# Low parts, sums of squares and gate sums of a two-layer hybrid block, moved from GpSimd to VectorE

## The chip, the cores and the metric

The kernel runs on one core of a Trainium2 chip. The metric is the device time of one launch, in microseconds (us): the median of three runs. The engines are called PE (TensorE: its matmuls; PEld is its weight load), DVE (VectorE), ACT (ScalarE), POOL (GpSimd) and SP (SyncE, which issues most of the transfers; a q behind an engine's name means its sequencer or queue).

## What is computed

One step of a diffusion transformer with two layers (D 1024, feed-forward width 2816) on 1024 latent tokens and 256 context tokens. Cut to the parts that the change touches:

```python
def rmsnorm(x, w):
    y = x * lax.rsqrt(jnp.mean(x * x, axis=-1, keepdims=True) + EPS)
    return y * w

def trunk_layer(x, mod, lp, ctx):
    sh1, sc1, g1, sh2, sc2, g2 = mod
    h = rmsnorm(x, lp['norm1_w']) * (1 + sc1) + sh1
    p = h @ lp['w_in']
    ...                                  # attention, RG-LRU scan, Hyena long convolution
    mix = jnp.concatenate([att, lru, hy], axis=-1)
    x = x + g1 * (mix @ lp['w_out'])
    h2 = rmsnorm(x, lp['norm2_w']) * (1 + sc2) + sh2
    x = x + g2 * ((jax.nn.silu(h2 @ lp['ffn_w1']) * (h2 @ lp['ffn_w3'])) @ lp['ffn_w2'])
    ...
```

The context tokens go through the same layer, with the same weights and a conditioning of their own.

## The kernel before, in words

**Products in two parts.** Every large matmul is made from three: each float32 operand is cut into a high part (rounded to fp32r) and a low part (what the rounding left), and `mm3` (L153 to L156) adds high by high (L154), high by low (L155) and low by high (L156) in PSUM. `split` (L158 to L161) makes the parts: ACT copies the high part (L160), then another engine subtracts it from the source and so writes the low part (L161). Which engine does that is the call's argument, DVE if there is none. The low part waits for the copy, and PE for both.

**Stages, in order, with the time of the profiled execution.** Loads, norm and modulation (0 to 106 us); `w_in` of layer 0 (to 400); filter spectra and Hyena (to 600); context mix and latent attention (to 958); `w_out` (to 1085); the quarters of the feed-forward operands (to 1130); ffn_up (to 1650); ffn_down (to 1955), with the norms of layer 1 in it; `w_in` of layer 1 (to 2200); Hyena and attention (to 2664); `w_out` (to 2800); quarters (to 2850); ffn_up (to 3350); ffn_down (to 3676).

**Weights.** `wtile` loads 128x1024 floats into a tile wst (3 buffers) and splits it into a tile whl (4 buffers; L161 on POOL). `w_in` and `w_out` use it.

**Norms.** `ss_add` squares on ACT (L360) and adds into two sums: one in three on DVE, the others on POOL (L362). `norm` scales each of the eight row blocks on DVE (L402); for even blocks ACT writes the high part with the bias and DVE the low part (L404, L405), for odd blocks ACT adds the bias, then copies the high part, and POOL subtracts (L160, L161).

**Feed-forward.** The products of the latents are done by a scheme of seven products of quarter size in place of eight. `quarters` (L510 to L554) forms the sums of the quarters of the normed latents on DVE (L538 to L547) and cuts each into its parts (`cut`, L526 to L528): of the 28 cuts, 12 are on DVE and 16 on POOL. In each of the 11 passes of `ffn_up` four weight tiles come in; each pair gives four splits of 128x1024 (w0, w1, wb, wa; L161 on POOL), DVE makes the weight sums between them (L628, L629, L633, L634), drains the products from PSUM (L622, L637 to L648) and computes the gates (L612, L614). At the end of a pass five sums of two gates (L656, on POOL) go to memory with two single gates (L657): sums 0, 3 and 6 through a tile gs with one buffer, 2 and 5 through slots of a tile e.

`ffn_down` has seven products of 11 passes each. A pass loads one or two 128x512 weight tiles (L694) and a gate sum (L700), adds two weights on DVE (L706), splits the result (A: L161 on POOL) and the gate sum (B: L161 on DVE), and PE does twelve matmuls of 512 columns. Passes with context work also split both weights (C, on POOL) and the context gates (gk, on DVE).

**Order.** The Tile framework's scheduler with its own timeline simulation sets the order on each engine (`TCARGS`). Each engine runs its instructions in that order; a semaphore holds one until what it reads is there and what it overwrites has been read. Buffers in pools come free in the same way. Line numbers after the change are lower by 4 from about L414 on, by 1 at L405.

## Time and profile before

| | |
|---|---|
| Median of three runs | 3681.47 us (3678.79 to 3682.36) |
| The profiled execution, its own time | 3678.18 us |
| Its span, first to last instruction | 3676.4 us |
| Mean granted clock of PE | 0.971 |
| Busy: PE, PEld | 3476.9 us (95%), 2758.4 us (75%) |
| Busy: DVE, ACT, POOL | 2331.1 us (63%), 1430.7 us (39%), 1444.6 us (39%) |
| L161 on POOL, output whl | 898.3 us in 463 instructions |

A busy share is an average over stages with different limits, and a busy PE is not PE at its peak. The time that can be won is in PE's gaps, and which engine ends a gap differs by stage. One core runs, so its span is the time but for some 2 us around it.

### The profile page before, as it was taken

What the parts mean: (1) busy time and instruction counts of PE and PEld (TensorE: products, weight loads), DVE (VectorE), ACT (ScalarE), POOL (GpSimd) and SP (SyncE); (2) the same over time, 40 slices, a digit from 0 to 9 for tenths busy, and PEclk for the clock granted to TensorE, in tenths of its full rate; (3) what the DMA queues carried; (4) which work ended last, traced back from release to release, by engine and by line L of the source; (5) the groups of instructions that cost most, each with busy time, mean ns of one, the idle gap of its engine ahead of it and who ended that gap; (6) DMA issues with size and microseconds to landing.
All of it is one profiled execution on the core that took longest, in us unless ns stands there. A gap on an engine that the chain in (4) does not pass through costs nothing.

```text
span 3676.4 us, 49838 instructions
## 1 busy us (share of the span) xinstructions
PE 3476.9 (95%) x18198; PEld 2758.4 (75%) x18198; DVE 2331.1 (63%) x4016; ACT 1430.7 (39%) x2347; POOL 1444.6 (39%) x940
## 2 busy tenths in 40 slices
PE   6989988999999999999999999989998999999998
PEld 3657776667777888887777778767686888888777
DVE  6544577887466655665685673777638556565666
ACT  4333333655342222224544542455524222222443
POOL 3333034110145555547654332310035555455664
PEclk7999998999999999999999999999998999999999
DMA  7565573310411222226675336430141222224667
GB/s 273 175 202 164 201 277 107 121 48 23 138 52 63 89 78 92 78 90 231 191 238 182 106 117 203 153 108 28 36 151 36 84 92 78 77 92 157 205 205 244
DMA packets 402331, 485.89 MB, mean 132 GB/s; under 512 B 38542, under 2 KB 251072, under 8 KB 398758
## 3 DMA queue, kind: packets, MB, share of 16 engines
q1 hardware_dynamic: 398950, 468.03, 38.7%
q0 software_dynamic: 3136, 14.68, 1.2%
q8 instruction: 143, 2.34, 0.3%
q14 instruction: 102, 0.84, 0.1%
HBM read 350.94 MB, written 131.67 MB: 131 GB/s over the span
## 4 chain that ended last, share of the span: by engine, by line
PE 60%; DVE 7%; DMA 6%; issue 5%; POOL 4%; ACT 2%; SPq 1%; DVEq 0%; POOLq 0%; ACTq 0%
PE pu L155 8%; PE pu L156 8%; PE pu L154 8%; PE pvo L966 4%; PE sps L931 4%; PE tps L947 4%; POOL whl L161 3%; PE puv L155 2%; PE puv L154 2%; PE puv L156 2%; PE ops L155 2%; PE ops L156 2%; PE ops L154 2%; DMA wst<-in_ffn_w_dram 2%; PE py L154 2%
## 5 line engine op out<-in xcount | busy, mean ns | idle before, releaser
L161 POOL TENSOR_TENSOR whl<-wst,whl 128x512 fp32r<-128x512 f32 (+1 forms) x463 | 898.3, 1950 | 866.5 <-ACT whl L160 833.6
L160 ACT ACTIVATE whl<-wst 128x512 fp32r<-128x512 f32 (+1 forms) x488 | 394.2, 825 | 846.2 <-PE pu L156 277.9
L154 PE MATMUL pu<-hq,whl 128*128 128x512 f32 x1232 | 489.6, 399 | 7.6 <-ACT hq L527 6.2
L156 PE MATMUL pu<-hq,whl 128*128 128x512 f32 x1232 | 488.8, 398 | 0.0
L154 PE MATMUL wps<-h,whl 128*128 128x512 f32 (+1 forms) x768 | 289.3, 377 | 2.9 <-ACT h L404 1.7
L155 PE MATMUL pu<-hq,whl 128*128 128x512 f32 x704 | 280.8, 399 | 8.4 <-POOL hq L528 4.8
L156 PE MATMUL wps<-h,whl 128*128 128x512 f32 (+1 forms) x768 | 287.9, 376 | 0.0
L155 PE MATMUL wps<-h,whl 128*128 128x512 f32 (+1 forms) x768 | 285.0, 371 | 1.7 <-POOL h L161 1.2
L154 PEld LDWEIGHTS pu<-hq,whl 128*128 128x128 f32 x1232 | 234.1, 190 | 63.0 <-ACT hq L527 8.1
L156 PEld LDWEIGHTS pu<-hq,whl 128*128 128x128 f32 x1232 | 234.4, 190 | 54.9
L154 PE MATMUL py<-whl 128*128 128x512 f32 x616 | 225.1, 399 | 14.3 <-ACT whl L160 8.9
L155 PE MATMUL py<-whl 128*128 128x512 f32 x616 | 228.5, 395 | 0.1
L156 PE MATMUL py<-whl 128*128 128x512 f32 x616 | 220.5, 394 | 1.6 <-POOL whl L161 1.6
L155 PE MATMUL pu<-hl,whl 128*128 128x512 f32 x528 | 210.9, 400 | 8.8 <-POOL hl L528 8.8
L934 ACT ACTIVATE pq<-pq,mn 128x1280 f32<-128x1280 f32 (+1 forms) x160 | 190.2, 1189 | 66.3 <-DVE pq L932 64.0
L947 PE MATMUL tps<-ident,pq 128*128 128x128 f32 x1344 | 198.7, 279 | 16.0 <-ACT pk L951 6.2
L156 PE MATMUL puv<-h,whl 128*128 128x256 f32 x704 | 200.4, 285 | 4.6 <-POOL whl L161 4.6
L154 PE MATMUL puv<-h,whl 128*128 128x256 f32 x704 | 200.1, 284 | 1.4 <-ACT whl L160 1.4
L706 DVE TENSOR_TENSOR wst<-wst 128x512 f32<-128x512 f32 x110 | 137.1, 1247 | 99.5 <-POOL whl L161 63.4
L155 PE MATMUL puv<-h,whl 128*128 128x256 f32 x704 | 200.0, 284 | 0.0
L947 PEld LDWEIGHTS tps<-ident,pq 128*128 128x128 f32 x1344 | 158.4, 143 | 52.4 <-DVE pk L949 18.1
L932 DVE TENSOR_SCALAR_CACHE_REDUCE pq<-sps,mn 128x512 f32<-128x512 f32 (+1 forms) x256 | 156.4, 612 | 46.7 <-PE sps L931 43.2
(355 smaller groups left out, 8038.1 us busy)
## 6 DMA issues: line engine op xcount, KB each, us to landing
wst<-in_ffn_w_dram SPq DMA_DIRECT2D x264, 256.0 KB
wst<-in_ffn_w_dram SPq DMA_DIRECT2D x88, 512.0 KB
wst<-in_w_mod_dram SPq DMA_DIRECT2D x68, 512.0 KB
gr<-gd_l SPq DMA_DIRECT2D x132, 256.0 KB
gd_l<-gs SPq DMA_DIRECT2D x66, 256.0 KB
wst<-in_w_in_dram SPq DMA_DIRECT2D x32, 512.0 KB
wst<-in_w_mod_dram SPq DMA_DIRECT2D x14, 1024.0 KB
gd_l<-g SPq DMA_DIRECT2D x44, 256.0 KB
```

The costliest lines, as they stand in the source:

```text
L154: mm(ps, wh, xh, start=first, stop=False)
L155: mm(ps, wh, xl, start=False, stop=False)
L156: mm(ps, wl, xh, start=False, stop=last)
L160: nc.scalar.activation(hi, src, AF.Copy)
L161: (eng or nc.vector).tensor_tensor(lo, src, hi.bitcast(F32), ALU.subtract)
L706: nc.vector.tensor_tensor(st[:, 0], st[:, 0], st[:, 1], op)
L931: nc.tensor.matmul(p, qx[:, ts], kt[:, h, k0:k0 + kn], start=h == 0, stop=h == 1)
L932: nc.vector.tensor_scalar(pt[:, k0:k0 + kn], p, -1.0, mn[:, c - 1:c] if c else BIG, ALU.mult, ALU.min, accum_out=mn[:, c:c + 1])
L934: nc.scalar.activation(pt, pt, AF.Exp, bias=mn[:, len(chunks) - 1:], scale=-1.0, accum_out=ls[:, t:t + 1])
L947: nc.tensor.transpose(ps[:, k, t], pq[t][:, (t0 + k) * 128:(t0 + k + 1) * 128], self.ident)
L966: nc.tensor.matmul(ob[64 * hd:64 * hd + 64, 0], vx[:, t], pk[:, t].rearrange("p t q -> p (t q)"), start=t == nkt - 1, stop=t == 0)
```

## The change

Everything that the norms, `w_in`, `w_out`, the quarters and both feed-forward stages did on GpSimd goes to VectorE: 463 low parts of weights (221 of 128x1024, 242 of 128x512), 32 low parts of odd norm blocks, 45 sums of squares, 32 cuts of quarters and 110 sums of gates, 682 instructions. The odd norm blocks now go the way of the even ones, so that ACT does one pass for each instead of two (32 fewer) and DVE's low part takes the bias in the same instruction. POOL keeps the filter, rotary, scan and convolution work and its transfers.

```diff
--- before.py
+++ after.py
@@ -359,7 +359,7 @@
                 sq = self.rows(list(xs.shape))
             nc.scalar.activation(sq, xs, AF.Square)
             h = 0 if d % three == 0 else 1
-            (nc.gpsimd if h else nc.vector).tensor_tensor(ss[:, h], ss[:, h], sq, ALU.add)
+            nc.vector.tensor_tensor(ss[:, h], ss[:, h], sq, ALU.add)
 
     def h_new(self, s, bi, hp):
         s.h[bi] = []
@@ -400,24 +400,20 @@
             A, B = self.nA[l][j][:, s.cond, d:d + 1], self.mod(l, s, 3 * j, d)
             t = tp.tile([128, N], F32, tag="ft", name="nt", bufs=FT)
             nc.vector.scalar_tensor_tensor(t, self.xs(s, bi, d), A, p2, ALU.mult, ALU.mult)
-            if d % 2 == 0:
-                nc.scalar.activation(hh, t, AF.Identity, bias=B)
-                nc.vector.scalar_tensor_tensor(hl, t, B, hh.bitcast(F32), ALU.add, ALU.subtract)
-            else:
-                nc.scalar.activation(t, t, AF.Identity, bias=B)
-                self.split(t, hh, hl, nc.gpsimd)
-
-    def wtile(self, src, shp=(8, 128), eng=None):
+            nc.scalar.activation(hh, t, AF.Identity, bias=B)
+            nc.vector.scalar_tensor_tensor(hl, t, B, hh.bitcast(F32), ALU.add, ALU.subtract)
+
+    def wtile(self, src, shp=(8, 128)):
         nc = self.nc
         st = self.wp.tile([128, *shp], F32, tag="wst", name="wst", bufs=SBUFS)
         nc.sync.dma_start(st, src)
         w = self.wp.tile([128, 2, *shp], F32R, tag="whl", name="whl", bufs=WBUFS)
-        self.split(st, w[:, 0], w[:, 1], eng or nc.gpsimd)
+        self.split(st, w[:, 0], w[:, 1])
         return w
 
-    def w_in_w(self, l, i, eng=None):
+    def w_in_w(self, l, i):
         m = MORDER[i]
-        return self.wtile(self.a["w_in"][l][:, m * 128:(m + 1) * 128].rearrange("(k p) m -> p k m", p=128), eng=eng)
+        return self.wtile(self.a["w_in"][l][:, m * 128:(m + 1) * 128].rearrange("(k p) m -> p k m", p=128))
 
     def w_in(self, l, pool, fill):
         nc = self.nc
@@ -431,7 +427,7 @@
             ws = []
             for i in g:
                 fill(i)
-                ws.append(self.w_in_w(l, i, nc.vector if l == 0 and i < 3 else None))
+                ws.append(self.w_in_w(l, i))
             es = {i: [] for i in g}
             for b in self.all:
                 s, bi, b0, N = b
@@ -514,7 +510,7 @@
         ha, hb, _ = hp
         b11, b21 = self.lat.x[0]
         b12, b22 = self.lat.x[1]
-        V, G = nc.vector, nc.gpsimd
+        V = nc.vector
 
         def pair(p, tag):
             t = p.tile([128, 2, 4, 512], F32R, tag=tag, name="hq")
@@ -523,34 +519,34 @@
         def low(tag):
             return cp.tile([128, 4, 512], F32R, tag=tag, name="hl")
 
-        def cut(x, hl, k, eng):
+        def cut(x, hl, k):
             nc.scalar.activation(hl[0][:, k], x[:, k], AF.Copy)
-            eng.tensor_tensor(hl[1][:, k], x[:, k], hl[0][:, k].bitcast(F32), ALU.subtract)
+            V.tensor_tensor(hl[1][:, k], x[:, k], hl[0][:, k].bitcast(F32), ALU.subtract)
 
         h11, h21 = pair(hb, "hl00"), pair(ha, "hl01")
         for k in range(4):
-            cut(b11, h11, k, G)
-            cut(b21, h21, k, V)
+            cut(b11, h11, k)
+            cut(b21, h21, k)
         t1, h22 = pair(hb, "hl10"), pair(hb, "hl11")
         a, b = pair(cq, "hq1")
         c = cq.tile([128, 4, 512], F32R, tag="hq4", name="hq4")
         for k in range(4):
             V.tensor_tensor(b11[:, k], b12[:, k], b11[:, k], ALU.subtract)
             V.tensor_tensor(b12[:, k], b22[:, k], b12[:, k], ALU.subtract)
-            cut(b11, t1, k, G)
+            cut(b11, t1, k)
         t3 = (a, low("xq00"))
         for k in range(4):
-            cut(b12, t3, k, V if k % 2 else G)
+            cut(b12, t3, k)
         for k in range(4):
-            cut(b22, h22, k, G)
+            cut(b22, h22, k)
             V.tensor_tensor(b22[:, k], b22[:, k], b11[:, k], ALU.subtract)
             V.tensor_tensor(b21[:, k], b22[:, k], b21[:, k], ALU.subtract)
         t2 = (b, low("xq10"))
         for k in range(4):
-            cut(b22, t2, k, V)
+            cut(b22, t2, k)
         t4 = (c, low("xq11"))
         for k in range(4):
-            cut(b21, t4, k, V if k % 2 else G)
+            cut(b21, t4, k)
         return h11, h21, h22, t4, t1, t2, t3
 
     def ffn_up(self, l, pool, cp, hq, mods):
@@ -559,13 +555,13 @@
         nc, a = self.nc, self.a
         H = NFF // 2
         lat, cs = self.lat, self.ctxs
-        V, G = nc.vector, nc.gpsimd
+        V = nc.vector
         h11, h21, h22, t4, t1, t2, t3 = hq
         e = cp.tile([128, 4, 512], F32, tag="xq01", name="e")
 
         def cut(st):
             w = self.wp.tile([128, 2, 8, 128], F32R, tag="whl", name="whl", bufs=WBUFS)
-            self.split(st, w[:, 0], w[:, 1], G)
+            self.split(st, w[:, 0], w[:, 1])
             return w
 
         def prod(w, x, b):
@@ -653,7 +649,7 @@
                 else:
                     n = q % 3
                     t = e[:, n + 1] if n else pool.tile([128, 512], F32, tag="gs", name="gs", bufs=1)
-                    G.tensor_tensor(t, ts[b[0]], ts[b[1]], op)
+                    V.tensor_tensor(t, ts[b[0]], ts[b[1]], op)
                 nc.sync.dma_start(lat.gd[q, p], t)
             for m in mods[2 * p:2 * p + 2]:
                 self.mods(*m, self.rows, lambda nm, shp=(128, 512): self.ps_l(nm, shp, "n"))
@@ -701,11 +697,11 @@
                 if ctx:
                     C = self.wp.tile([128, 2, 2, 512], F32R, tag="whl", name="whl", bufs=WBUFS)
                     for j in range(2):
-                        self.split(st[:, j], C[:, j, 0], C[:, j, 1], nc.gpsimd)
+                        self.split(st[:, j], C[:, j, 0], C[:, j, 1])
                 if len(src) == 2:
                     nc.vector.tensor_tensor(st[:, 0], st[:, 0], st[:, 1], op)
-                self.split(st[:, 0], A[:, 0], A[:, 1], nc.gpsimd)
-                self.split(br, B[:, 0], B[:, 1], nc.vector)
+                self.split(st[:, 0], A[:, 0], A[:, 1])
+                self.split(br, B[:, 0], B[:, 1])
                 if n < 2 and 0 < p < 9:
                     if p == 1:
                         self.x_new(lat, 1 - n, xp, 2)
```

**Quarters.** POOL before, layer 0 (hq and hl are the cut operands, xq their sources):

```order
L528 TENSOR_TENSOR hq_9603<-xq00_8660,hq_9603 128x512 [waits Activation_49] x4
...
L528 TENSOR_TENSOR hq_9622<-xq11_8683,hq_9622 128x512 [waits Activation_49] x3
L528 TENSOR_TENSOR hq_9621<-xq00_8660,hq_9621 128x512 [waits Activation_49] x2
...
L528 TENSOR_TENSOR hl_9641<-xq10_8682,hq_9623 128x512 [waits Activation_49]
...
L528 TENSOR_TENSOR hl_9675<-xq01_8661,hq4_9624 128x512 [waits DVE_49]
```

DVE now, at the same place:

```order
L161 TENSOR_TENSOR whl_9854<-wst_9850,whl_9854 128x1024 [waits DMAHW1_49,Activation_49]
L534 TENSOR_TENSOR xq00_8648<-xq10_8670,xq00_8648 128x512 [waits Activation_49] x2
L524 TENSOR_TENSOR hq_9606<-xq11_8671,hq_9606 128x512 [waits Activation_49]
...
L535 TENSOR_TENSOR xq10_8670<-xq11_8671,xq10_8670 128x512 [waits DVE_49]
L524 TENSOR_TENSOR hq_9605<-xq00_8648,hq_9605 128x512 [waits Activation_49] x2
...
L524 TENSOR_TENSOR hl_9625<-xq10_8670,hq_9607 128x512 [waits Activation_49] x3
...
L524 TENSOR_TENSOR hl_9659<-xq01_8649,hq4_9608 128x512 [waits Activation_49] x3
```

The cuts of POOL's rows now stand between DVE's sums of the quarters (L534, L535, before L538, L539), with one weight split ahead of them.

**ffn_up.** DVE now, at the turn of a pass in layer 0 (gs and e<-g are the sums of gates, whl the weight splits, L608 and L610 the gates, L618 and L633 draining products):

```order
L652 TENSOR_TENSOR gs<-g 128x512 [waits DMAHW5_49,DVE_49]
L610 SCALAR_TENSOR_TENSOR g<-g,e 128x512 [waits DVE_49] x2
L652 TENSOR_TENSOR e<-g 128x512 [waits DVE_49]
L652 TENSOR_TENSOR gs<-g 128x512 [waits DMAHW6_49]
L652 TENSOR_TENSOR e<-g 128x512 [waits DMAHW7_49,DVE_49]
L618 TENSOR_TENSOR g<-pu,e 128x512 [waits DVE_49,DMAHW0_49,PE_49,Activation_49]
L161 TENSOR_TENSOR whl<-wst,whl 128x1024 [waits Activation_49]
L652 TENSOR_TENSOR gs<-g 128x512 [waits DMAHW0_49]
L608 SCALAR_TENSOR_TENSOR g<-e,g 128x512 [waits Activation_49]
L161 TENSOR_TENSOR whl<-wst,whl 128x1024 [waits DMAHW3_49,Activation_49]
```

The five sums and two of the next pass's splits, which stood in POOL's queue, now stand in DVE's; the second and third gs wait there for the store of the one before (DMAHW).

**ffn_down.** DVE now, product 4 of layer 0 (gr<- rows split the gate sum, wst<- rows the weights; L702 adds two weights, before L706):

```order
L702 TENSOR_TENSOR wst_16096<-wst_16096 128x512 [waits DMAHW4_49,DMAHW3_49]
L161 TENSOR_TENSOR whl_15982<-wst_15983,whl_15982 128x512 [waits Activation_49]
L402 SCALAR_TENSOR_TENSOR nt_15536<-x_c_480,nA1_0_116,nps2_15519 128x256 [waits DVE_49]
L161 TENSOR_TENSOR whl_16095<-gr_16099,whl_16095 128x512 [waits DMAHW2_49,Activation_49]
...
L702 TENSOR_TENSOR wst_16119<-wst_16119 128x512 [waits DMAHW7_49,DMAHW6_49]
L161 TENSOR_TENSOR whl_16095<-wst_16096,whl_16095 128x512 [waits Activation_49]
```

The low part of a pass's weights (whl 15982, then 16095) stands behind the add of the next pass, which waits for that pass's weights (DMAHW); before, it stood in POOL's queue, where no add stands.

## Rows read from the trace of the kernel before

**Rows 1.** The page's head and its section 1: busy time, share of the span, instructions.

```profile
span 3676.4 us, 49838 instructions
PE 3476.9 (95%) x18198; PEld 2758.4 (75%) x18198; DVE 2331.1 (63%) x4016; ACT 1430.7 (39%) x2347; POOL 1444.6 (39%) x940
```

**Rows 2.** Stretches: from:to, length, busy us by engine, PE's clock, DMA share, GB/s.

```profile
1085.00:1130.00 45.00, 31.08 (x121) 23.98 (x121) 40.27 (x51) 21.77 (x35) 25.04 (x15) 0.77 0.02 6
1130.00:1650.00 520.00, 520.00 (x2704) 442.25 (x2703) 311.70 (x351) 129.62 (x169) 269.38 (x134) 1.00 0.26 85
...
1800.00:1955.00 155.00, 144.91 (x629) 116.48 (x629) 124.33 (x164) 75.08 (x135) 96.42 (x68) 0.98 0.69 226
...
2020.00:2200.00 180.00, 164.18 (x818) 133.98 (x818) 125.80 (x169) 92.06 (x135) 56.69 (x26) 0.94 0.32 104
2800.00:2850.00 50.00, 36.58 (x145) 27.87 (x144) 44.58 (x53) 24.98 (x40) 28.35 (x16) 0.80 0.05 16
...
3500.00:3676.00 176.00, 163.01 (x740) 131.26 (x738) 117.76 (x144) 71.44 (x124) 91.48 (x63) 1.00 0.68 222
```

**Rows 3.** Groups by line and form on POOL: busy us, mean ns | idle before, releasers.

```profile
L161 POOL TENSOR_TENSOR whl<-wst,whl 128x1024 fp32r<-128x1024 f32 x221 | 550.7, 2493 | 627.5 <-ACT whl L160 603.4 <-issue 20.5 <-DMA fe_l<-e 3.6
L161 POOL TENSOR_TENSOR whl<-wst,whl 128x512 fp32r<-128x512 f32 x242 | 347.7, 1454 | 239.0 <-ACT whl L160 230.2 <-DMA gr<-gd_c 5.2 <-issue 1.3
```

**Rows 4.** Timeline, ffn_up of layer 0, DVE and POOL: start us, us, instruction.

```profile
1400.97 0.69 DVE L614 SCALAR_TENSOR_TENSOR g<-g,e 128x512 f32<-128x512 f32 x1
...
1402.99 2.84 POOL L161 TENSOR_TENSOR whl<-wst,whl 128x1024 fp32r<-128x1024 f32 x1
...
1403.50 2.88 DVE L614 SCALAR_TENSOR_TENSOR g<-g,e 128x512 f32<-128x512 f32 x1
```

**Rows 5.** Groups by line and form on DVE, with their idle time and its releasers.

```profile
L612 DVE SCALAR_TENSOR_TENSOR g<-e,g 128x512 f32<-128x512 f32 x88 | 142.0, 1614 | 24.8 <-ACT e L611 24.8
L706 DVE TENSOR_TENSOR wst<-wst 128x512 f32<-128x512 f32 x110 | 137.1, 1247 | 99.5 <-POOL whl L161 63.4 <-DMA wst<-in_ffn_w_dram 35.8
...
L637 DVE TENSOR_TENSOR e<-pu,e 128x512 f32<-128x512 f32 x44 | 30.4, 692 | 229.1 <-PE pu L156 229.1
```

**Rows 6.** One tile's instructions (mst, in w_out): duration ns min/median/max, first and last start.

```profile
L161 DVE TENSOR_TENSOR h<-mst,h x16: 1209/1226/3390, 671.2 to 2685.5; 128x1024 fp32r<-128x1024 f32 x16
```

**Rows 7.** Timeline of the quarters, layer 0, DVE and POOL.

```profile
1087.83 5.36 DVE L507 SCALAR_TENSOR_TENSOR xq<-xq,nA,nps 128x512 f32<-128x512 f32 x8 [1.57 <-PE nps L389]
...
1095.35 10.21 POOL L528 TENSOR_TENSOR hq<-xq,hq 128x512 fp32r<-128x512 f32 x6 [1.07 <-ACT hq L527]
...
1114.48 3.81 DVE L528 TENSOR_TENSOR hl<-xq,hq 128x512 fp32r<-128x512 f32 x6
...
1120.97 2.97 POOL L528 TENSOR_TENSOR hl<-xq,hq 128x512 fp32r<-128x512 f32 x2
```

**Rows 8.** PE's waits, 1085 to 1130 us: us in total, times, longest.

```profile
PE pu L155 <- POOL hl L528: 4.3, 1, 4.3
PE pu L154 <- ACT hq L527: 3.4, 2, 2.9
PE pu L155 <- POOL hq L528: 2.5, 1, 2.5
```

**Rows 9.** PE's longest waits in ffn_down of layer 0, 1800 to 1955 us.

```profile
PE pyc L156 <- DVE gk L161: 3.9, 2, 2.3
PE py L154 <- DVE x_l L733: 2.9, 1, 2.9
```

**Rows 10.** PE's longest wait in w_in of layer 1, 2020 to 2200 us.

```profile
PE qp L799 <- ACT qrx L795: 8.8, 2, 6.1
```

**Rows 11.** Timeline before that wait ended, DVE and POOL.

```profile
2163.26 2.34 POOL L1090 TENSOR_TENSOR xp<-xp,gl 128x1024 f32<-128x1024 f32 x1 [2.00 <-DVE qrr L176]
...
2163.31 2.33 DVE L173 TENSOR_TENSOR qrt<-qrr 128x20 f32<-128x20 f32 x1
```

**Rows 12.** The chain that ended last, end of ffn_up of layer 1: start us, us, what.

```profile
3382.26 4.91 DMA gd_l<-gs
```

## The prediction

> **What bounds the kernel now.** I read the page's busy times first. TensorE is busy 3476.9 of 3676.4 us [rows 1], so this change, which takes no matmul away, can win at most the other 199.5 us. VectorE is at 63% and GpSimd at 39%, but the stretches show that this average hides three kinds of stage [rows 2]. In ffn_up (1130 to 1650) TensorE is busy in all of its 520 us: nothing can be won there, and 269 us of GpSimd work is hidden. In the two quarters stages (1085 to 1130, 2800 to 2850) VectorE is busy 40.3 of 45 and 44.6 of 50 us while TensorE has 13 to 14 us idle in each, at a granted clock of 0.77 and 0.80. In ffn_down and the second w_in TensorE misses 10 us of 155, 13 us of 176 and 16 us of 180.
>
> Next I looked at what the moved instructions cost now [rows 3]: a weight split takes GpSimd 2493 ns (128x1024) or 1454 ns (128x512). That is only their own time. The timeline shows what they do to VectorE [rows 4]: a gate step takes 0.69 us at 1400.97, but 2.88 us at 1403.50, where it runs beside a GpSimd split of 2.84 us and ends with it. The groups show that this is the rule in the feed-forward stages [rows 5]: L612 takes 1614 ns on average (x88), the weight sums of L706 1247 ns (x110). The same split as on GpSimd, 128x1024, takes VectorE 1209 ns at least and 1226 at the median [rows 6]. So VectorE's 63% holds waiting for GpSimd. At 0.69 us for each, the excess of L612 alone is 88 x 0.92 = 81 us and that of L706 110 x 0.56 = 62 us; over the groups of two-input operations I count some 320 us.
>
> **The sum, part by part.** All of it is against the profiled execution, span 3676.4, own time 3678.18 us, which lies 3.3 us under the median of the runs, 3681.47; I apply the same difference to the median.
>
> VectorE's load. Added: 221 x 1.21 + 242 x 0.69 + 110 x 0.69 us is 510 us, and the 109 norm, square and quarter operations at up to 0.69 us bring at most 75 more: about 580 us. Less 320 us of excess, VectorE goes from 2331 to about 2590 us, 70% of the span. On average that fits; the question is the stages.
>
> Quarters, two stages. GpSimd's last cut ends at 1120.97 + 2.97 = 1123.94; VectorE does six cuts in 3.81 us, 0.635 each, where GpSimd takes 10.21 us for six [rows 7]. In the new order VectorE does, from 1087.83 on, the rescaling (5.36 us), a weight split (1.21), 16 sums and 20 cuts (36 x 0.635 = 22.9): 29.4 us, done at 1117.2, 6.7 us before GpSimd is done now. TensorE waits 4.3 and 2.5 us for GpSimd's cuts there and 3.4 us for copies that wait for VectorE's sums [rows 8], so up to 10 us are to be had, and none if it then waits for VectorE's cuts at the same times. The first low part of the third product, on which the 4.3 us rest, stands behind the weight split and some 22 operations: 1087.8 + 5.4 + 1.2 + 22 x 0.635 = 1108.4, ready at 1109 against 1112.4 now. I take 3 us a stage, **-6 us**; bounds -20 and 0.
>
> The rule that speaks against this part: the Trainium skill, Perfetto Trace Analysis, section Optimizing Scalar/DVE Operations, says that if VectorE is saturated, moving work from it, even to GpSimd, may make sense, and adds that the port that the two share may undo it. Read by its first half, 16 cuts on a VectorE that is 90% busy would be an addition; this is the third rival, below. Its second half is what the 2.88 us row shows.
>
> ffn_up. Per pass VectorE gets eight splits and five sums, 8 x 1.21 + 5 x 0.69 = 13.1 us, on 28 of 47 us busy now (311.7 of 520, 11 passes). That is 41 us even if nothing is given back. TensorE covers it: it has no gap to lose or win, and VectorE waits 229.1 us in 42 times for its products at L637, 5.45 us each [rows 5]. **0 us**. The cover fails if the sums' stores are slow (second rival).
>
> ffn_down, two stages. From 1800 to 1955 GpSimd's 68 instructions become 68 x 0.69 = 47 us on VectorE, which has 124 of 155 us busy. Given back: 62 us at L706 and about as much at the other splits, over the 630 us of both stages, so some 31 us in this stretch. VectorE comes to 140 of 155 us, 90%. TensorE's longest waits here are ended by VectorE operations, 3.9 us for the context gates' split and 2.9 us for a residual update [rows 9], both behind operations stretched by GpSimd. Half of these 6.8 us in each layer: **-7 us**; bounds -23 (all of TensorE's idle time, 10 and 13 us) and +36 (first rival).
>
> w_in of layer 1. TensorE waits 8.8 us for ACT's rotary step, 6.1 of it at once [rows 10]. Ahead of that a small step of the inverse root takes VectorE 2.33 us, but the GpSimd operation beside it, L1090, is one that stays [rows 11], so this part remains. What is left are splits of 1.21 in place of 2.49 us and one ACT pass less for each odd norm block: **-2 us**; bounds -6 and +3.
>
> w_out, twice. The first split stands ahead of the product and takes 2493 - 1209 ns less: **-2.5 us**; bounds -4 and 0. Front and w_in of layer 0, with the norms: **-2 us**; bounds -4 and +3, since VectorE's draining of products now stands behind splits of 1.21 us. The 45 squares' sums go in among work that is not waited for: 0.
>
> Together -19.5 us: **3662 us** on the median (3658.7 on the profiled execution).
>
> **Rivals.**
> 1. *The adds' waits hold the low parts (slower).* In ffn_down the low part of a pass's weights now stands in VectorE's queue behind the next pass's add, and that add waits for its transfer; GpSimd's queue had no such add. VectorE waited 35.8 us in 28 times for weights at L706 [rows 5]. It decides where the wait is longer than the lead that the low part has over TensorE. If all 28 waits reach TensorE, 35.8 us come in and the 7 us are not won: -12.5 + 35.8 = +23, **3705 us**. For it: the stretch loads 226 GB/s with VectorE at 90%. Against it: shorter splits free the weight buffers sooner, so that transfers start earlier.
> 2. *The gate sums wait for their stores (slower).* In ffn_up the second and third gs wait in VectorE's queue for the store of the one before, with splits behind. A store landed 4.91 us after its issue at the end of the stage [rows 12]; three operations of 0.69 us (2.1) and then two and a split (2.6) stand between, so VectorE would stand still for 2.8 + 2.3 = 5.1 us a pass, just under the 5.45 us that it waits at L637. From a landing of 5.1 us on, each further us costs up to two, in 22 passes: at 6.1 us +44, **3706 us**. Against it: over the whole stage only 85 GB/s are moved [rows 2], and 4.91 us is a value from its busy end.
> 3. *VectorE bound in the quarters.* If its operations there are long of themselves, 16 cuts x 0.635 = 10.2 us a stage come on top: +20 - 13.5 = +6.5, **3688 us**. Against it: six cuts in 3.81 us as soon as GpSimd pauses [rows 7].
> 4. *All of it was hidden.* The stretched operations end, but TensorE's gaps are kept by transfers, copies and the order: within a few us of **3681 us**.
> 5. *More is won.* Most of the waits named end, and the higher clock returns sooner in the quarters: 16 there, 16 in ffn_down, 3 in w_in, 6 elsewhere, -41: **3640 us**.
>
> **How the numbers follow.** Forecast 0.45 (3652 to 3674); more is won 0.15; hidden 0.13; quarters bound 0.07; adds hold low parts 0.13; stores 0.07. A measurement of this kernel can tell some 0.2%, 7.4 us. So faster 0.45 + 0.15 = 0.60, same 0.13 + 0.07 = 0.20, slower 0.13 + 0.07 = 0.20. The range goes from 3636, just under rival 5, to 3698, which leaves out most of rivals 1 and 2 and little else; the forecast's own bounds lie within it.
>
> **What would show it.** Right: L612 and L706 near 0.69 us; VectorE near 2590 us busy, GpSimd near 260 (1444.6 less the moved groups); no change from 1130 to 1650; quarters shorter by about 3 us each, with TensorE's wait for the low parts under 2 us; fewer waits for the context gates. Wrong: L702 (L706 before) waiting for DMA with TensorE's L156 waiting for VectorE's split of weights right after (rival 1); a gate sum that waits for DMA for over 5 us, and TensorE under 520 us busy in ffn_up (rival 2); VectorE's cuts over 0.8 us apiece (rival 3). A two-input VectorE operation that stays at 1.2 us without GpSimd would break the whole sum.

## The result, and the profile after

The changed kernel takes 3642.05 us (median of four runs, 3640.13 to 3644.62) beside 3680.13 for the kernel before: ratio 0.9898, 95% interval 0.9884 to 0.9913. That is 38 us less, about twice the 19.5 that were forecast; the time lies inside the range. Head and section 1 of the page of the changed kernel, beside [rows 1]:

```profile
span 3638.4 us, 49311 instructions
PE 3471.0 (95%) x18198; PEld 2759.9 (76%) x18198; DVE 2439.1 (67%) x4698; ACT 1423.9 (39%) x2315; POOL 269.7 (7%) x258
```

VectorE took over 682 instructions and is only 108 us busier. Why is in its groups by form (to be read beside [rows 5] and, for the first two, [rows 3]; L608 and L702 were L612 and L706):

```profile
L161 DVE TENSOR_TENSOR whl<-wst,whl 128x1024 fp32r<-128x1024 f32 x224 | 276.4, 1235 | 250.6 <-ACT whl L160 247.0 <-PE fp L1170 2.2
L161 DVE TENSOR_TENSOR whl<-wst,whl 128x512 fp32r<-128x512 f32 x264 | 175.4, 687 | 66.3 <-ACT whl L160 65.2
...
L702 DVE TENSOR_TENSOR wst<-wst 128x512 f32<-128x512 f32 x110 | 75.6, 688 | 38.9 <-DMA wst<-in_ffn_w_dram 38.9
...
L608 DVE SCALAR_TENSOR_TENSOR g<-e,g 128x512 f32<-128x512 f32 x88 | 58.8, 688 | 0.0
...
L652 DVE TENSOR_TENSOR gs<-g 128x512 f32<-128x512 f32 x66 | 45.5, 690 | 54.9 <-DMA gd_l<-gs 54.9
```

In the feed-forward stages, where GpSimd now has nothing to do, the splits, sums and gates of 128x512 all take 0.69 us. TensorE's busy time fell by 6 us, and its gaps went from 199.5 to 167.4 us.

Where the time went is best seen by stages, cut in TensorE's sequence. The first w_in, both w_out, ffn_up and ffn_down begin with the first matmul of their product; both w_in and the first ffn_down end as their last matmul begins, the second ffn_down with the last matmul of all; the quarters end as the 101st matmul of ffn_up begins. Of each kernel this is the one profiled execution, in us:

| | front | w_in 0 | mix 0 | w_out 0 | quarters 0 | ffn_down 0 | w_in 1 | mix 1 | w_out 1 | quarters 1 | ffn_down 1 |
|---|---|---|---|---|---|---|---|---|---|---|---|
| before | 87.5 | 333.8 | 517.3 | 139.2 | 56.3 | 300.9 | 292.7 | 415.7 | 127.3 | 55.9 | 301.8 |
| after | 92.1 | 342.0 | 519.3 | 135.5 | 54.7 | 286.0 | 276.4 | 413.1 | 124.9 | 54.6 | 292.2 |
| p_down | 87.2 | 331.9 | 516.9 | 139.1 | 56.3 | 292.6 | 296.6 | 415.0 | 125.8 | 57.0 | 295.9 |
| p_q | 87.3 | 334.4 | 520.7 | 139.2 | 49.4 | 301.0 | 295.8 | 412.5 | 127.4 | 48.9 | 303.3 |
| p_up | 86.7 | 339.1 | 517.5 | 139.1 | 56.4 | 298.3 | 283.2 | 412.7 | 125.7 | 56.7 | 298.9 |
| f_first | 91.2 | 337.3 | 517.7 | 138.9 | 56.2 | 301.6 | 282.2 | 415.5 | 127.3 | 53.2 | 301.8 |
| p_win1 | 87.2 | 334.6 | 519.5 | 139.2 | 56.3 | 301.3 | 278.6 | 412.9 | 127.3 | 56.2 | 302.5 |
| m_norm | 88.1 | 336.4 | 514.9 | 135.6 | 51.3 | 292.1 | 276.4 | 413.2 | 124.6 | 52.5 | 293.2 |
| all_q2 | 89.2 | 343.7 | 517.6 | 135.6 | 51.9 | 289.4 | 279.4 | 416.0 | 125.9 | 51.9 | 293.6 |
| all_dmyw | 92.6 | 346.9 | 516.7 | 135.5 | 54.6 | 286.9 | 288.4 | 412.7 | 125.7 | 53.1 | 293.0 |

The two ffn_up, left out, take 520.5 to 521.5 us in all of these except f_first (523.3 in layer 1, for 2.6 less in its quarters). Stage times scatter. The front and the first w_in took 419.1 to 425.8 us together in five kernels with the same order of matmuls there (before, p_down, p_q, p_up, p_win1), and 429.2 to 439.5 in the six with the changed kernel's order (after, all_dummy, all_dmy256, all_q1, all_q2 and all_dmyw). Kernels that do the same work on the same engines in another stage agree better: within some 2 us in the quarters and 4 in ffn_down and the second w_in.

So ffn_down won 24.4 us, the second w_in 16.3, w_out 6.1, the quarters only 2.8; the front and the first w_in lost 12.9.

### The profile page after: what moved, and what is told of

It is laid out like the page before. It is cut to its first block, busy times and chain, and to the rows that moved or that the text cites. A ratio compares the mean times of both kernels' runs of the same rounds, so it can differ in the third digit from the quotient of the medians.

```text
span 3638.4 us, 49311 instructions
## 1 busy us (share of the span) xinstructions
PE 3471.0 (95%) x18198; PEld 2759.9 (76%) x18198; DVE 2439.1 (67%) x4698; ACT 1423.9 (39%) x2315; POOL 269.7 (7%) x258
## 4 chain that ended last, share of the span: by engine, by line
PE 62%; DVE 9%; DMA 7%; issue 2%; ACT 2%; POOL 0%; SPq 0%; DVEq 0%; ACTq 0%; POOLq 0%
PE pu L155 8%; PE pu L156 8%; PE pu L154 8%; PE pvo L962 4%; PE sps L927 4%; PE tps L943 3%; DMA wst<-in_ffn_w_dram 3%; PE py L154 2%; PE py L156 2%; PE puv L155 2%; PE py L155 2%; PE puv L154 2%; PE puv L156 2%; PE ops L155 2%; PE ops L156 2%
## 5 line engine op out<-in xcount | busy, mean ns | idle before, releaser
L161 DVE TENSOR_TENSOR whl<-wst,whl 128x512 fp32r<-128x512 f32 (+1 forms) x488 | 451.8, 939 | 316.9 <-ACT whl L160 312.1
L155 PE MATMUL py<-whl 128*128 128x512 f32 x616 | 225.7, 394 | 0.4 <-DVE whl L161 0.4
L154 PE MATMUL py<-whl 128*128 128x512 f32 x616 | 219.0, 395 | 3.5 <-DVE x_l L729 2.4
L156 PE MATMUL py<-whl 128*128 128x512 f32 x616 | 214.0, 393 | 2.0 <-DVE whl L161 2.0
L943 PEld LDWEIGHTS tps<-ident,pq 128*128 128x128 f32 x1344 | 157.0, 142 | 47.2 <-DVE pk L945 12.9
L154 PEld LDWEIGHTS wps<-h,whl 128*128 128x128 f32 x768 | 149.5, 195 | 36.4 <-issue 8.5
```

Of the source, the lines that this page charges most:

```text
L154: mm(ps, wh, xh, start=first, stop=False)
L155: mm(ps, wh, xl, start=False, stop=False)
L156: mm(ps, wl, xh, start=False, stop=last)
L161: (eng or nc.vector).tensor_tensor(lo, src, hi.bitcast(F32), ALU.subtract)
L943: nc.tensor.transpose(ps[:, k, t], pq[t][:, (t0 + k) * 128:(t0 + k + 1) * 128], self.ident)
```

## The experiments

Where one part moves alone, the diff is the part's own lines of the change, and the rest is as before.

**ffn_down alone (p_down).**

```diff
-                        self.split(st[:, j], C[:, j, 0], C[:, j, 1], nc.gpsimd)
+                        self.split(st[:, j], C[:, j, 0], C[:, j, 1])
...
-                self.split(st[:, 0], A[:, 0], A[:, 1], nc.gpsimd)
+                self.split(st[:, 0], A[:, 0], A[:, 1])
```

> Only the weight splits of ffn_down move to VectorE, all else as before. Theory A (GpSimd's two-input operations hold up VectorE's, so what ffn_down gains is won there alone): ffn_down gains 14 to 16 us in layer 0 and 8 to 10 in layer 1, as in the whole change, the other stages stay within 2 us: time about 24 us under before, 3656. Rival B (part of the gain needs the norms and sums of squares of that stage to move too): under 12 us in all, over 3668.

3670.73 us, ratio 0.9969 (0.9958 to 0.9981). The time is on B's side. In the profiled execution, which at 3664.09 us lies 6.6 under the median, ffn_down won 8.3 and 5.9 us: less than A's and, for ffn_down alone, more than B's 12, and more than the forecast's 3.5 each. L706 fell to 694 ns. The other 10 us of the whole change came only with the rest (3 of them in m_norm, which still leaves the norms).

**GpSimd's work put back beside it (all_dummy, all_dmy256).** Nothing of the computation changes; a scratch result is added:

```diff
                 self.split(br, B[:, 0], B[:, 1])
+                hi = A[:, 0].bitcast(F32)
+                for _ in range(3 if ctx else 1):
+                    nc.gpsimd.tensor_tensor(dmy, hi, hi, ALU.add)
```

> The whole change, and in every pass of ffn_down GpSimd adds the weights' high part to itself into a scratch tile that nobody reads (three times in passes with context work): GpSimd's operations of before, without a consumer. Theory A (contention): VectorE's two-input operations of 128x512 beside them go from 0.69 to 1.0 to 1.3 us on average, and ffn_down gives back 12 to 24 us: 3654 to 3666. Rival B (GpSimd was only slow on the way from the weights to TensorE): durations may rise, but the time stays within 5 us of the changed kernel, 3637 to 3647.

3723.07 us, ratio 1.0120 (1.0105 to 1.0135): 81 us over the change, 42 over the kernel before. ffn_down went to 333.6 and 336.2 us. Nobody reads what these operations write, but each holds the weight tile that it reads until it is done; what that costs by itself comes out with the next kernel. VectorE and GpSimd in the timeline of all_dummy:

```profile
1760.66 4.42 DVE L161 TENSOR_TENSOR whl<-wst,whl 128x512 fp32r<-128x512 f32 x3
...
1760.34 4.19 POOL L708 TENSOR_TENSOR dmy<-whl 128x512 f32<-128x512 f32 x3 [1.96 <-ACT whl L160]
```

Three of VectorE's splits take 4.42 us beside three of GpSimd's operations in 4.19, where three in a row without GpSimd take 1.90 (VectorE's sums at 1119.11 in the changed kernel): they run in turn. The Trainium skill, SBUF — State Buffer, section SBUF: two separate sides, says the same: the two engines share one pair of ports, and whichever of a VectorE operation with two inputs in SBUF and a GpSimd operation that reads SBUF starts first holds it for the whole instruction. These rows agree.

That it costs more than before fits VectorE's one split more in each pass. If so, what counts is the sum of both engines' two-input work against TensorE's pass; the second kernel halves GpSimd's part.

> As all_dummy, with scratch operations of half the size, 128x256, in the same number. Theory A (VectorE's two-input operations and GpSimd's run one after the other, and what counts is whether their sum fits under TensorE's pass): per pass without context 3 x 0.60 + 0.80 = 2.6 us fits under TensorE's 12 x 0.23 = 2.8, so those lose nothing; with context 6 x 0.60 + 3 x 0.80 = 6.0 us are a little over 24 x 0.23 = 5.5: 5 to 30 us over the changed kernel, 3647 to 3672. Rival B (each GpSimd operation costs time in proportion to its length): 0.57 to 0.63 of the 81 us of all_dummy, 3688 to 3693.

3659.74 us, ratio 0.9941 (0.9925 to 0.9958): 18 us over the change, inside A's 5 to 30, not 49. But A has it in part by luck. ffn_down took 300.2 and 304.8 us, 26.8 more in the two together, and 17.8 of these fall in its first product, which has no context work: 39.3 and 39.8 us in place of 30.6 and 30.7. In all_dummy it took as long, 39.5 and 39.1. GpSimd and ACT at its start in all_dmy256, layer 0:

```profile
1668.13 6.55 POOL L708 TENSOR_TENSOR dmy<-whl 128x256 f32<-128x256 f32 x7 [721.09 <-DVE ng L663]
...
1668.77 3.23 ACT L160 ACTIVATE whl<-wst 128x512 fp32r<-128x512 f32 x6 [11.22 <-POOL dmy L708]
```

The first scratch operations start late and hold their weight tiles till then, and ACT's next copy waits 11.2 us for one. That is a price of the scratch operations, not of contention. With the context matmuls taken out that came forward into the first product (some 4 and 3 us), I estimate it at 14 us in each of the two kernels. What is left in ffn_down is some 13 us for operations of 128x256 and 77 for those of 128x512: half the work costs a sixth. So the price is not in proportion. A budget that costs from where the pass is full fits that, but no run shows where the cost begins.

**The second w_in alone (p_win1).**

```diff
-                ws.append(self.w_in_w(l, i, nc.vector if l == 0 and i < 3 else None))
+                ws.append(self.w_in_w(l, i, nc.vector if l == 1 or i < 3 else None))
```

> Only the weight splits of the second layer's w_in move to VectorE. Theory A (GpSimd's splits there push its scan and convolution work into the chain that normalises the queries): the second w_in gains 12 to 17 us by itself, time 3664 to 3669. Rival B (that gain needs the norms' or ffn_down's part): under 5 us, over 3675.

3667.21 us, ratio 0.9959 (0.9944 to 0.9974), the stage 14.1 us shorter: A's number. The wait of 6.1 us of [rows 10] is gone; the longest on the queries is 2.1. But the order changed with it: by the trace 212 of TensorE's 1367 places in that stage are others than before, so this run does not separate the engine from the order.

**ffn_up alone (p_up).**

```diff
-            self.split(st, w[:, 0], w[:, 1], G)
+            self.split(st, w[:, 0], w[:, 1], V)
...
-                    G.tensor_tensor(t, ts[b[0]], ts[b[1]], op)
+                    V.tensor_tensor(t, ts[b[0]], ts[b[1]], op)
```

> Only ffn_up's weight splits and gate sums move to VectorE. Theory A (TensorE has no gap there and VectorE's stalls for the stores are covered): both ffn_up stages within 1 us of before, the time within 4 us, 3677 to 3685. Rival B (the gate sums' waits for their stores reach TensorE): 10 us or more slower, over 3690.

3656.02 us, ratio 0.9939 (0.9924 to 0.9955): outside both theories. ffn_up itself is unchanged, as A says, but the time fell by 24 us (15 in the profiled execution). The stages that got shorter are ffn_down, by 5.5, and above all the second w_in, by 9.5, of which no instruction had changed engine. The scheduler had put that stage in another order (by the trace, 274 of TensorE's 1367 places there). The first w_in took 5.3 us longer in this execution, with the order and the engines of before: that is scatter.

**The first norm alone (f_first).** The norm's low parts and sums as in the change, for layer 0's first norm only.

```diff
-            (nc.gpsimd if h else nc.vector).tensor_tensor(ss[:, h], ss[:, h], sq, ALU.add)
+            (nc.gpsimd if h and three != 2 else nc.vector).tensor_tensor(ss[:, h], ss[:, h], sq, ALU.add)
...
-            if d % 2 == 0:
+            if d % 2 == 0 or l == j == 0:
```

> Before, with only the very first norm (layer 0, ahead of w_in) and its sums of squares on VectorE. Theory A (this is the part of the change that loses time, by the order of layer 0's first 430 us): 6 to 12 us slower than before, 3687 to 3693, with the front and w_in of layer 0 5 us or more longer together. Rival B (the loss needs the weight splits in VectorE's queue as well): within 4 us of before.

3676.32 us, ratio 0.9992 (0.9983 to 1.0001). Front and first w_in are 7.2 us longer, as A says; the total, 3.4 us under before, is B's number. The second w_in hides the loss, for it is again 10.5 us shorter, in the same order, place by place, as p_up's. p_q, which keeps the order of before there but for 4 places, takes 295.8. So the order alone, with the splits still on GpSimd, is worth 10 us.

What the order does shows on the small steps of the inverse root for the queries, on VectorE, which end in ACT's rotary step (qrx). First step (qv) and scan (lh), before, after the change, and in p_up:

```profile
2156.45 2.35 DVE L1076 TENSOR_TENSOR_SCAN lh<-lc,cols,ld 128x1024 f32<-128x1024 f32 x1
2158.72 0.15 DVE L788 TENSOR_SCALAR qv<-qp 128x20 f32<-128x20 f32 x1
...
2140.20 0.17 DVE L784 TENSOR_SCALAR qv<-qp 128x20 f32<-128x20 f32 x1
2145.23 2.35 DVE L1072 TENSOR_TENSOR_SCAN lh<-lc,cols,ld 128x1024 f32<-128x1024 f32 x1
...
2151.29 0.17 DVE L788 TENSOR_SCALAR qv<-qp 128x20 f32<-128x20 f32 x1
```

Before, the first step stands behind the scan, 202.5 us into the stage. After the change it stands ahead of it, at 189.5, and in p_up too, at 193.5 (scan at 198.4). TensorE's wait at the end of these steps was 6.1 us before, and is 0.2 after and 1.9 in p_up and f_first.

**GpSimd's work put back in the second w_in (all_dmyw).** The computation is unchanged; the spent staging tile of layer 1's weights is overwritten:

```diff
+        if dmy:
+            hi = w[:, 0].bitcast(F32)
+            nc.gpsimd.tensor_tensor(st, hi, hi, ALU.add)
```

> The whole change, and for every weight tile of the second w_in GpSimd adds the high part to itself into the spent staging tile: the GpSimd operations of before, 128x1024, that nobody waits for but the staging buffer. The scheduler's order in that stage shifts with them (170 of 1295 matmul places). Theory A (GpSimd's splits cost the second w_in its 14 to 17 us, by contention and by pushing back GpSimd's scan and convolution work): the stage goes from 276 back to 285 to 293 us, time 3650 to 3660. Rival B (the order chosen by the scheduler made the gain, as in f_first and p_up, which leave those splits on GpSimd and gain 10 there): 276 to 282 us, time 3642 to 3648.

3652.28 us, ratio 0.9916 (0.9900 to 0.9933); the stage went from 276.4 to 288.4 us: A's numbers. TensorE's waits there, where the rotary step is back (3.3 us in the changed kernel, 8.8 before) and the norm's low parts on VectorE are new (0.7 in the changed kernel), at 1.05 us apiece where they take 0.75 without the scratch operations:

```profile
PE qp L798 <- ACT qrx L794: 7.0, 2, 3.5
PE wps L155 <- DVE h L404: 5.2, 8, 1.6
```

The order moved too (by the trace 211 of 1368 places against the changed kernel), so the 12 us are not all contention for certain. No run has the order of before without GpSimd's work, or the changed kernel's order with it. Together the runs say that the stage can be slow for either reason.

**The norms (p_front, m_norm).** p_front moves the odd norm blocks and the sums of squares alone, m_norm everything else.

> Only the norms' low parts and the sums of squares move, the weight splits, cuts and gate sums stay on GpSimd. Theory A (this part reorders TensorE's sequence in layer 0 and so costs the 13 us that the whole change lost by the end of layer 0's w_in): the last w_in product of layer 0 comes 8 to 17 us later than before. Rival B (that loss comes from weight splits in VectorE's queue): it comes within 3 us of before. The time then is before plus 8 to 17 us by A, less whatever the second w_in gives (0 to 16 us); within 4 us of before by B.

3692.18 us, ratio 1.0026 (1.0015 to 1.0037). The first w_in ends 7.0 us later, 4.7 from the front and 2.3 from w_in: a little under A's lower end, and slower in all. That is of the profiled execution, the fastest of ten at 3677.71 us (the other nine took 3683.7 to 3695.2), so where the 12 us of the median went is not known.

> The whole change but for the norms' low parts and the sums of squares, which stay as before. Theory A (the loss in layer 0's w_in belongs to the norms' part): the 13 us by the end of layer 0's w_in are gone; if the second w_in's gain of 16 us stays, 3629, if it goes with the norms, 3645. Rival B (the loss belongs to the weight splits): layer 0's w_in still ends 10 us or more late.

3631.23 us, ratio 0.9869 (0.9854 to 0.9883): faster than both kernels. The loss by the end of the first w_in shrinks from 12.9 to 3.2 us and the second w_in keeps its gain, A with 3629. So the norms' part costs some 10 us there.

**The first w_in's splits back (m_norm_win0).** `w_in_w` as in p_win1, on m_norm.

> As m_norm, and the weight splits of layer 0's w_in stay on GpSimd too (but for the first three, as before). Theory A (in layer 0's w_in VectorE's queue has other work to do, and the splits there cost 2 to 4 us): 3 us less than m_norm, about 3628. Rival B (those splits gain or lose nothing): within 2 us of m_norm's 3631.

3650.11 us, ratio 0.9923 (0.9906 to 0.9939): neither. The first w_in is 0.8 us shorter, but the second takes 285.3 us and the mix after it 6.5 more; its order differs from m_norm's in 292 places by the trace, and ten modulation products moved into it.

**The quarters (p_q, m_q0, all_q1, m_q1, all_q2, m_q2).** p_q moves the cuts alone.

> Only the cuts of the quarters move to VectorE. Theory A (contention with GpSimd's cuts stretches VectorE's sums): 2 to 5 us less in each of the two stages, 3672 to 3677. Rival B (VectorE is full there, and 16 cuts of 0.6 us more are an addition): 2 us or more longer in each, 3685 or more.

3666.70 us, ratio 0.9966 (0.9954 to 0.9978): 6.9 and 7.0 us less, more than A's 5, and the opposite of B. In the whole change it was 1.6 and 1.2. TensorE's longest waits in the quarters, layer 0, of the changed kernel, beside [rows 8]:

```profile
PE puv L156 <- DVE whl L161: 5.4, 1, 5.4
PE pu L155 <- DVE hl L524: 3.9, 1, 3.9
```

A new wait, for a weight split, has taken the place of those removed. VectorE's timeline shows where that split stands:

```profile
1102.15 5.35 DVE L503 SCALAR_TENSOR_TENSOR xq<-xq,nA,nps 128x512 f32<-128x512 f32 x8 [3.41 <-PE nps L389]
1107.42 1.22 DVE L161 TENSOR_TENSOR whl<-wst,whl 128x1024 fp32r<-128x1024 f32 x1
```

ACT's copy was ready before 1102.82, when TensorE began on it; the low part stood behind eight rescalings. I put the split back on GpSimd, with `eng` as an argument of `cut`, twice missing it: m_q0 moved the first split of the pass, q1 the second, and the wait stayed at 5.4 us.

> As m_norm, and the first weight split of each ffn_up goes back to GpSimd, since in the changed kernel TensorE waits 5.4 us for it behind the rescaling in VectorE's queue. Theory A (that wait is the one that took the place of those removed in the quarters): 2 to 5 us less in each quarters stage, 3621 to 3627. Rival B (VectorE's 29 us of rescaling, sums and cuts set the end of the stage whatever comes first): within 2 us of m_norm in all, 3629 to 3633.

> The whole change, but the second weight split of each ffn_up (the first pass's w1, the one for which TensorE waits 5.4 us in the quarters; m_q0 had moved the one before it) stays on GpSimd. Theory A (this wait took the place of those that the change removed there): each quarters stage 3 to 6 us shorter, 3630 to 3636. Rival B (VectorE's 29 us there set its end): each within 1.5 us, 3639 to 3645.

> m_norm with the same second split on GpSimd. Theory A: quarters 2 to 5 us shorter in each layer than m_norm's 51.3 and 52.5, 3621 to 3627. Rival B: 3629 to 3633.

m_q0 3632.89 us (0.9870; 0.9855 to 0.9884), all_q1 3635.59 (0.9878; 0.9862 to 0.9895), m_q1 3628.57 (0.9866; 0.9851 to 0.9880): their quarters are within 3 us of the kernels that they start from, on both sides. That all_q1's time lies in A's range is luck, since its quarters moved by 0.1 and 1.5 us only. The third try is the right one:

```diff
-                w0 = cut(raw[0])
+                w0 = cut(raw[0], G if p == 0 and part else V)
```

> The whole change, but the split on which TensorE waits 5.4 us in the quarters stays on GpSimd: it is the first one of the first pass's second half (ffn_w3); m_q0 and all_q1 had moved its two neighbours, and the wait stayed. Theory A (its place behind eight rescalings in VectorE's queue costs that wait): the wait goes to 2 us or less, as in p_q, each quarters stage is 3 to 6 us shorter than all_q1's 54.6 and 53.1, time 3626 to 3633. Rival B (VectorE's 29 us there set the stage's end): the wait moves to the cuts, each stage within 1.5 us.

> m_norm with the same split on GpSimd. Theory A: quarters 2 to 5 us shorter in each layer than m_norm's 51.3 and 52.5, 3620 to 3627. Rival B: 3627 to 3633.

TensorE's waits in the quarters of all_q2, layer 0:

```profile
PE pu L155 <- DVE hl L524: 2.9, 1, 2.9
...
PE puv L156 <- POOL whl L161: 1.9, 1, 1.9
```

The wait falls to 1.9 us, as A says, and both quarters to 51.9 us, 2.8 under the changed kernel's in each, and 2.7 and 1.2 under all_q1's; less than A's 3 to 6. In m_q2 they are 50.1 and 49.7 us, 1.2 and 2.8 under m_norm's. The time, 3639.66 us (0.9890; 0.9875 to 0.9904) and for m_q2 3630.93 (0.9859; 0.9842 to 0.9876), shows no gain that could be told from the changes of other stages: the first misses A's 3626 to 3633, the second is B's.

**All norms but the first (b2).** m_q0, and f_first's two conditions turned round (`three == 2`, and `l or j`): every norm but the first goes to VectorE.

> As m_q0, and all norms and sums of squares but those of the very first norm go to VectorE too. Theory A (the norms' part gains about 6 us in ffn_down of layer 0 and loses only in the first norm): 4 to 8 us under m_q0, about 3618. Rival B (any norm part reorders layer 0's front): 3 us or more over m_q0.

3632.86 us, ratio 0.9864 (0.9849 to 0.9879): the same as m_q0, neither theory's number. Its front and first w_in took 424.9 us, in the order of m_norm. The five kernels with that order (m_norm, m_q0, m_q1, m_q2, b2) took 423.1 to 426.2 us there, the six with the first norm on VectorE as well 429.2 to 439.5. So the norms' loss is the first norm's, some 10 us. The 6 us by which the changed kernel's ffn_down of layer 0 beats m_norm's (286.0 and 292.1) did not come back here (291.9), and stay open.

m_norm, b2, m_q1 and m_q2 cannot be told apart: about 3630 us, 1.3% under the kernel before.

## Why the prediction was off, point by point

The mechanism held: GpSimd's operations stretch VectorE's, and without them TensorE waits less. The sizes did not hold. ffn_down and the second w_in won more than their own bounds allowed (24.4 us against 23, 16.3 against 6), and the front with the first w_in lost 12.9 us where the bound was 3. The total lies 2 us from rival 5, *more is won*, with its chance of 0.15. But rival 5 has 16 us in the quarters, 16 in ffn_down, 3 in w_in and 6 elsewhere, where 2.8, 24.4, 16.3 and a loss of 5.5 were measured: that its total fits is luck.

**VectorE's load** was to be 2590 us and is 2439. The 580 us added were right (588 by the durations in the changed kernel). Group by group, by durations before and after, GpSimd had cost VectorE 425 us, not 320; some 25 of these are small operations of at most 128x20, of which [rows 11] shows one. The other 55 us are overlap: eight operations of 0.69 us in a row show 5.11 us busy, not 5.5, and the sum went by 0.69 for each.

**Quarters**, -6 forecast, -2.8 measured. That VectorE's own sequence would take 29.4 us held: it ran from 1102.15 to 1131.17. The step that failed is its start, taken at 1087.83 from before. Against the stage's start the rescaling came 3.1 us later. 1.3 of these are on VectorE, where the first block's cuts, moved there as well, now stand among the steps of the second block's norm. The other 1.8 are a longer wait for TensorE's transposes (L389), which stand behind matmuls of ffn_up: from 1094.2 to 1098.6 us the granted clock was 0.50 there, the lower of its two levels (1.2 and 2.4 GHz), after a wait and sixteen matmuls of two columns; in the same place before it was 1.00. And TensorE then waited 5.4 us for the weight split behind the rescaling. I had listed it in the order and given it 1.21 us, but not asked who waits for it.

The rule of the Trainium skill (Perfetto Trace Analysis, Optimizing Scalar/DVE Operations), behind rival 3, misled by its first half here and was right by its second: p_q won 14 us in the quarters on an engine that was 90% busy, since much of the busy time was waiting.

**ffn_up**, 0 forecast, -0.6 measured. The stores made VectorE wait 54.9 us in 22 times, 2.5 for each pass, where up to 5.1 were allowed for; TensorE never saw it (rival 2).

**ffn_down**, -7 forecast, -24.4 measured: the mis-sized term. I took half of two waits. TensorE's longest waits in layer 0 of the changed kernel, beside [rows 9]:

```profile
PE py L156 <- DVE whl L161: 2.0, 2, 1.9
PE pyc L156 <- DVE gk L161: 1.9, 2, 1.0
```

All of TensorE's gaps fell, from 15.1 to 5.4 us in layer 0 and 13.0 to 5.7 in layer 1. Of the waits put down to ACT's copies (4.7 and 4.2 us before), 3.2 and 1.6 us had a weight sum on VectorE one step back, most of these stretched to over 1.6 us. The other 7.5 us are no gaps but TensorE's busy time in the same matmuls: 285.7 to 280.5 us and 288.8 to 286.5, with the granted clock up from 0.99 to 1.00 in both.

Rival 1 was there, VectorE waited 38.9 us for weights at L702, and it did not decide: TensorE waited 2.0 us for the weights' low parts in layer 0.

**w_in of layer 1**, -2 forecast, -16.3 measured: the second mis-sized term. "The GpSimd operation beside it, L1090, is one that stays, so this part remains" was the false step. It stays, but not beside these steps: in the changed kernel L1086, the same operation, began at 2151.50, and the last of the steps was done at 2150.82, since they began 13 us earlier in the stage, ahead of the scan. In p_up, with the splits still on GpSimd, they stand ahead of the scan as well, and the wait is 1.9 us. So it is mainly the order on VectorE that ended the wait of 6.1 us. No term of mine allowed for the scheduler ordering a stage anew; by f_first and p_up that alone is worth 10 us. The other 6 of the 16.3 are not separated: p_win1 and all_dmyw fit a price of GpSimd's work, but their orders differ as well.

**Front and w_in of layer 0**, -2 forecast, +12.9 measured: the wrong sign. The two stages before, and after the change:

```profile
0.00:87.50 87.50, 59.51 (x251) 30.84 (x251) 53.14 (x123) 43.50 (x82) 28.54 (x25) 0.75 0.79 281
87.50:421.25 333.75, 319.58 (x1530) 232.24 (x1528) 158.50 (x351) 114.54 (x216) 100.10 (x53) 0.97 0.54 175
...
0.00:92.10 92.10, 67.81 (x254) 32.49 (x255) 59.44 (x135) 42.09 (x80) 17.15 (x14) 0.68 0.77 276
92.10:434.17 342.07, 324.83 (x1526) 238.13 (x1524) 165.51 (x373) 110.23 (x206) 53.71 (x30) 0.94 0.52 168
```

TensorE's gaps are 3.7 us less in the front and 3.1 more in w_in. The loss is busy time, 13.5 us more in nearly as many matmuls, and the granted clock is lower in both stages, 0.68 after 0.75 and 0.94 after 0.97. The step that failed is the term of -2 us for front and w_in of layer 0 with the norms: by b2 and the kernels beside it, moving the first norm costs some 10 us. f_first, where it moves alone, has some 7. The order of the matmuls moves with it; why the clock is lower in that order stays open. The clock in the front also differs between executions of the same order: all_dmy256 had 0.78 there and took 87.8 us.

**w_out**, -2.5 forecast, -6.1 measured. In layer 1 TensorE's wait for the weights' low part went from 1.7 to 0.5 us, as priced. In layer 0 the wait that went, 1.8 us, was for a split of the mixed rows that VectorE did before too. Where the rest comes from is not traced.

## What to carry to other kernels

Before moving work off GpSimd, add up what its operations take from VectorE: price each two-input operation at its minimum, not its mean, and ask per pass whether both engines' sum fits under TensorE. An operation that stays on an engine is not an operation that stays in its place; when a queue empties, what is left in it runs earlier. An operation added as a test, without a consumer, still holds what it reads. And where a scheduler orders the work, a change in one stage can reorder another, so read the order of every stage, and check a gain in total by stages before crediting it to the part that was moved.

## What the runs showed of the hardware

The cost of GpSimd's work beside VectorE's is no fixed price: beside some 14 us, by my estimate, that their held tiles cost, 242 scratch operations of 128x256 made the two ffn_down some 13 us longer, as many of 128x512 some 77. The operations that drain PSUM did not change, 740 ns before and 745 after for the residual update in ffn_down of layer 0.

The granted clock can differ between kernels in the same place of the work: 1.00 before and 0.50 after for a stretch of 4.4 us in the quarters of layer 0.
